# The order of every engine's instructions written by a list schedule

## The chip, the cores and the metric

The kernel runs on one core of one Trainium2 chip. The metric is the device time of one execution in microseconds; of three executions the median is given, with the lowest and the highest. The engines are PE (matmuls and transposes), DVE (the vector engine), ACT (the scalar engine), POOL (GpSimd) and SP, whose queue starts the loads and stores. Each runs its own instructions in its own order and waits for the others by semaphores.

## What is computed

The reference is one layer of a decoder trunk, on 512 tokens of width 1024, all in float32:

```python
mod = silu(c) @ ada_w + ada_b
sh1, sc1, g1, sh2, sc2, g2 = split(mod, 6)
h = rms_norm(x, pre_norm_mix) * (1 + sc1) + sh1
z = h @ w_in                  # g_rnn, x_rnn, q, and keys and values: compressed, selected, window; gates
rnn = gelu(g_rnn) * rg_lru(conv4(x_rnn))                   # two block-diagonal gates, a scan over the tokens
att = nsa_attention(q, ...)                                # 8 heads, 2 groups of keys, three soft-maxes per head
y = concat(rms_norm(rnn), rms_norm(att)) @ w_out
x = x + (1 + g1) * rms_norm(y, post_norm_mix)
h = rms_norm(x, pre_norm_mlp) * (1 + sc2) + sh2
y = square(relu(h @ w_ff1)) @ w_ff2                        # width 4096
x = x + (1 + g2) * rms_norm(y, post_norm_mlp)
```

## The kernel before

**Tiles.** Tokens are four tiles of 128. A float32 product of weight and activation is done as three matmuls (`mm3`, line 762): both are split into a high and a low part of float32r, and the product of the two low parts is left out. A weight is loaded raw, its high part is copied by ACT or DVE and its low part subtracted by DVE or POOL (`split_f32`, line 399; `hi_` and `lo_` in the profile). PSUM's eight banks are given out by use: two `f`, three `s`, one `pv`, two `tp` (line 440 on).

**Stages.** The first wave (`first_wave`, line 689) normalizes x and computes the first 768 columns of the projection, the keys. Then come, mixed with one another: the remaining projections x, g, v and q and the compression (`projections`, `compress`, `values`), the recurrent gates (`gates`, line 913) with their sigmoids, exponentials, roots and four scans on DVE (`vector_work`, line 1060; tiles `r`), the attention by units of a query tile and a pair of heads (`att_scores`, line 1194: scores in `s` banks, a maximum on DVE into `mx`, an exponential on ACT into `p`; `att_values`, line 1249: transposes into `tp` and `pt`, products in the `pv` bank, a division on DVE into `tmp`, sums on POOL into `att`), the modulation vectors from ada_w as multiply-adds on DVE (`ada_cols`, line 1041; `ar` rows of 512 KB, `accT`), and the output projection (banks `f`, weights `hi_o`, activations `h` of the recurrent part and `Q` of the attention). A query tile's attention ends in `att_finish` (line 1297), its residual in `residual` (line 1161). Then y is normalized and transposed for the MLP (`turn_h`, line 1331), whose first four up tiles are done in two halves of the tokens (`up_first`, line 1358: half 0 in banks `pv` and `s` before half 1). The other 28 up tiles (`up`) take 24 matmuls each in an `f` bank, ACT's relu and POOL's square. `down_all` keeps eight banks, and its last four tiles of the inner width go token tile by token tile, each ending in a norm and a store.

**Who sets the order.** Every instruction passes through the class `Clocks` (lines 51 to 270), whose helpers are the profile's lines: `mm` L220, `turn` L223, `act` L234, `elem` L255 for DVE and POOL, `zero` L258, `load` L270. It keeps an estimated clock for each engine and, for each tile, when it was last written and read. Each stage is a generator of instructions (`Stream`); `run_streams` (line 291) asks at every step which stream could go first by those clocks, and gives it a step. The clocks also choose between ACT and DVE for copies and between DVE and POOL for low parts. From line 760 on, the instructions so given are only recorded with cost, predecessors and estimated start (`put`, line 147), and three calls of `flush` (line 118) emit them: after attention, after the transition, and at the end. `flush` goes through one heap for all engines, whose key is 0.7 times an instruction's estimated start less 0.3 times the longest chain behind it (`TAIL`). PE's estimated cost is doubled in a window behind an idle one (`pace`, line 203).

The first wave is emitted inside `tc.manual_schedule()` (lines 488 to 759): there each engine's order is the order of emission. Behind line 759 the framework's own scheduler goes over what is emitted and may order it otherwise.

A tile belongs to a ring of its tag with a fixed number of slots (`tile`, line 69); a new tile takes the oldest slot. `ar` has 2, raw weights `RAW_BUFS` = 4. `Weights` (line 316) loads ahead of splits and splits ahead of use.

## Time and profile before

| | |
|---|---|
| times of three runs | 700.12, 702.43, 703.76 us |
| median | 702.43 us |
| span of the profiled execution, first to last instruction | 700.8 us |
| mean granted TensorE clock in it | 0.978 |
| PE busy | 654.4 us, 93% |
| DVE, ACT, POOL busy | 414.2, 267.6, 157.9 us |
| read from HBM | 82.43 MB, 121 GB/s over the span |

The profiled execution's own time is its span, 700.8 us; the median of the runs is 1.6 us above it. PE is busy in nearly all of the span, so time can only be lost where PE waits or works at a lowered granted clock. A row of a timeline gives start and duration in us, engine, line, operation, tile written from tiles read, and in brackets the idle time before it with what ended it. A matmul's record lasts longer than its share of the engine, since successive ones overlap; distances from start to start are the price. A float32 matmul shows as two records.

### The profile page before, as it was taken

The numbers are of one execution on the slowest core, as the hardware profiler recorded it, in microseconds if no ns is written. First come the engines' busy times: TensorE is split into PE (matmuls) and PEld (weight loads), VectorE is DVE, ScalarE is ACT, GpSimd is POOL, SyncE is SP. The second block draws the span as 40 slices with busy tenths as digits, with TensorE's granted clock in tenths as the row PEclk, the third lists the DMA queues.
The fourth block names the chain that finished last, engine by engine and source line by source line (L and its number), as shares of the span: only waits on it lengthen the run. The fifth ranks groups of instructions, "written<-read, shape, count | busy, mean of one in ns | idle before, by whom it ended". The sixth has DMA issues, their size and how long they took to land.

```text
span 700.8 us, 9072 instructions
## 1 busy us (share of the span) xinstructions
PE 654.4 (93%) x3350; PEld 543.0 (77%) x3350; DVE 414.2 (59%) x788; ACT 267.6 (38%) x553; POOL 157.9 (23%) x148
## 2 busy tenths in 40 slices
PE   3888899894999999998899999999999999999995
PEld 3666788474888889897898888888888888888884
DVE  5998974678688856684895374343353333333334
ACT  4335424584686665565441111111122332222221
POOL 4232010337225201222234343333410000000001
PEclk9999999897999999999999999999999999999999
DMA  8985668642435510001556353432323222223102
GB/s 272 271 249 158 181 206 235 206 130 85 132 111 157 201 35 27 1 0 55 157 151 180 90 151 93 118 91 91 102 97 101 91 91 90 91 91 96 55 18 102
DMA packets 89971, 85.10 MB, mean 121 GB/s; under 512 B 5172, under 2 KB 71876, under 8 KB 89928
## 3 DMA queue, kind: packets, MB, share of 16 engines
q1 hardware_dynamic: 89928, 84.54, 39.6%
q8 instruction: 26, 0.43, 0.3%
q14 instruction: 17, 0.14, 0.1%
HBM read 82.43 MB, written 2.10 MB: 121 GB/s over the span
## 4 chain that ended last, share of the span: by engine, by line
PE 49%; DVE 1%; ACT 0%; issue 0%; POOL 0%; DVEq 0%; POOLq 0%
PE f L220 28%; PE s L220 11%; PE tp L220 7%; PE pv L220 4%; DVE r L255 1%; PE tp L223 0%; ACT ar L234 0%; POOL stat L255 0%; ACT r L234 0%; DVEq L1483 0%; POOLq L1483 0%; DVE h2l L255 0%; DVE stat L255 0%
## 5 line engine op out<-in xcount | busy, mean ns | idle before, releaser
L220 PE MATMUL f<-h,hi_f 128*128 128x512 f32 x224 | 83.4, 393 | 0.0
L220 PE MATMUL f<-h,lo_f 128*128 128x512 f32 x224 | 82.7, 389 | 0.0
L220 PE MATMUL f<-h2l,hi_f 128*128 128x512 f32 x224 | 82.6, 389 | 0.0
L255 POOL TENSOR_TENSOR fT<-fT 128x512 f32<-128x512 f32 x32 | 57.9, 1812 | 107.3 <-ACT fT L234 107.3
L255 DVE TENSOR_TENSOR fl<-fT,fh 128x512 fp32r<-128x512 f32 x28 | 19.3, 690 | 88.1 <-ACT fh L234 88.1
L234 ACT ACTIVATE fT<-f 128x512 f32<-128x512 f32 x28 | 16.8, 600 | 126.1 <-PE f L220 126.1
L234 ACT ACTIVATE fh<-fT 128x512 fp32r<-128x512 f32 x28 | 17.7, 632 | 105.1 <-PE f L220 103.3
L255 POOL TENSOR_SCALAR stat<-stat 128x1 f32<-128x1 f32 (+1 forms) x21 | 7.8, 373 | 218.7 <-DVE stat L255 182.3
L255 DVE CAST hi_f<-raw_f 128x1024 fp32r<-128x1024 f32 x24 | 18.0, 749 | 63.5 <-PE f L220 63.5
L234 ACT ACTIVATE p<-p,mx 128x32 f32<-128x32 f32 (+4 forms) x96 | 45.3, 473 | 26.1 <-DVE mx L255 25.9
L255 DVE SCALAR_TENSOR_TENSOR accT<-ar,sil,accT 128x512 f32<-128x512 f32 x56 | 50.0, 892 | 6.5 <-DMA ar<-in_ada_w 5.9
L255 DVE TENSOR_TENSOR lo_d<-raw_d,hi_d 128x1024 fp32r<-128x1024 f32 x32 | 40.2, 1255 | 15.7 <-ACT hi_d L234 15.3
L220 PEld LDWEIGHTS f<-h,hi_f 128*128 128x128 f32 x224 | 42.1, 188 | 9.1 <-issue 0.5
L220 PEld LDWEIGHTS f<-h2l,hi_f 128*128 128x128 f32 x224 | 42.0, 188 | 9.1 <-issue 0.5
L220 PEld LDWEIGHTS f<-h,lo_f 128*128 128x128 f32 x224 | 42.1, 188 | 8.8
L220 PEld LDWEIGHTS pv<-V,pt 128*128 128x128 f32 x320 | 44.8, 191 | 2.9 <-ACT pt L234 0.5
L220 PE MATMUL pv<-V,pt 128*128 128x64 f32 x320 | 44.4, 260 | 0.2 <-ACT pt L234 0.2
L220 PE MATMUL s<-K,Q 128*128 128x288 f32 (+4 forms) x128 | 35.3, 346 | 9.5 <-DVE mx L255 9.5
L255 DVE TENSOR_TENSOR lo_f<-raw_f,hi_f 128x1024 fp32r<-128x1024 f32 x30 | 40.7, 1357 | 3.9 <-ACT hi_f L234 1.3
L223 PE MATMUL tp<-ident,p 128*128 128x128 f32 (+1 forms) x192 | 40.6, 279 | 0.7 <-DVE h L255 0.7
L220 PE MATMUL s<-hi_d,fh 128*128 128x512 f32 x84 | 33.3, 396 | 0.0
L220 PE MATMUL s<-hi_d,fl 128*128 128x512 f32 x84 | 33.3, 396 | 0.0
(259 smaller groups left out, 1607.4 us busy)
## 6 DMA issues: line engine op xcount, KB each, us to landing
ar<-in_ada_w SPq DMA_DIRECT2D x32, 512.0 KB, 5.4
raw_f<-in_w_ff SPq DMA_DIRECT2D x32, 512.0 KB, 4.1
raw_d<-in_w_ff SPq DMA_DIRECT2D x32, 512.0 KB, 3.2
p<-in_ada_w SPq DMA_DIRECT2D x32, 256.0 KB, 3.8
raw_o<-in_w_out SPq DMA_DIRECT2D x8, 512.0 KB, 4.3
r<-in_x SPq DMA_DIRECT2D x7, 512.0 KB
raw_a<-in_w_in SPq DMA_DIRECT2D x8, 320.0 KB, 5.2
raw_x<-in_w_in SPq DMA_DIRECT2D x4, 512.0 KB
```

What stands on the lines that cost most here:

```text
L220: lambda: self.nc.tensor.matmul(out, lhs, rhs, start=start, stop=stop))
L223: self.issue("pe", out.free_size() / 1175, [out], [src], lambda: self.nc.tensor.transpose(out, src, ident))
L234: lambda: self.nc.scalar.activation(out, src, func, scale=scale, bias=bias, **kw))
L255: self.issue(eng, cost, outs, ins, lambda: fn(out, *args, **kw))
```

## The change

The framework's scheduler is shut out for the whole program: `start_ctx.close()` moves from behind the first wave to the end. `flush` becomes an event-driven list schedule. For each engine (PE, ACT, DVE, POOL, DMA) it keeps a time; at each step the engine that can start first takes, of its instructions whose predecessors are done by the plan, the one with the longest chain behind it. A result is seen by another engine after a lag (`LAG`: 0.2 us from PE, 0.15 from the others, 2.0 for a load). On ACT an instruction that needs another table is put back by `TABLE_COST` = 40 us of chain, and costs 1.3 us more. The plan's times go on from one flush to the next. The costs are set anew, `pace` goes. A raw tile is `live` from its load to its split (or drop), and a new tile takes the first slot in the ring that isn't live; only an instruction that writes a tile depends on the slot's previous user. `run_streams`, the streams, the matmuls and the sizes of tiles stay. In the built order ACT loads its tables 14 times, and a few low parts (`lo_x2`, `lo_v1`) pass from POOL to DVE. In the changed file the helpers' lines are mm L252, turn L255, act L266, elem L287, zero L290, load L304.

```diff
-WINDOW = 4096 / 1200.0
+LAG = {"pe": 0.2, "act": 0.15, "dve": 0.15, "pool": 0.15, "dma": 2.0}
+TABLE_COST = 40.0
...
+        self.emitted = 0
+        self.live = set()
+        self.real = dict.fromkeys(("pe", "act", "dve", "pool", "dma"), 0.0)
+        self.real_table = None
+        self.fin = {}
...
-            old = ring.pop(0)
+            old = ring.pop(next(k for k, v in enumerate(ring) if v not in self.live))
...
     def flush(self):
-        nodes, self.nodes = self.nodes, []
-        tail = [0.0] * len(nodes)
-        for k in range(len(nodes) - 1, -1, -1):
+        first, nodes = self.emitted, self.nodes
+        self.emitted = n = len(nodes)
+        tail, left = {}, {}
+        after = {k: [] for k in range(first, n)}
+        for k in range(n - 1, first - 1, -1):
             eng, cost, prev = nodes[k][:3]
-            tail[k] += cost
+            tail[k] = tail.get(k, 0.0) + cost
+            left[k] = 0
             for j in prev:
-                lag = (SYNC if nodes[j][0] != eng else 0.0) + (DMA_LAT if nodes[j][0] == "dma" else 0.0)
-                tail[j] = max(tail[j], tail[k] + lag)
-        left = [0] * len(nodes)
-        after = [[] for _ in nodes]
-        for k, (_, _, prev, _, _, _) in enumerate(nodes):
-            left[k] = len(prev)
-            for j in prev:
-                after[j].append(k)
-        key = [(1 - TAIL) * start - TAIL * tail[k]
-               for k, (_, _, _, _, start, _) in enumerate(nodes)]
-        heap = [(key[k], k) for k in range(len(nodes)) if not left[k]]
-        heapq.heapify(heap)
-        while heap:
-            _, k = heapq.heappop(heap)
+                if j >= first:
+                    left[k] += 1
+                    after[j].append(k)
+                    tail[j] = max(tail.get(j, 0.0), tail[k] + self.lag(nodes[j][0], eng))
+        ready = {k: max([0.0] + [self.fin[j] + self.lag(nodes[j][0], nodes[k][0]) for j in nodes[k][2] if j < first])
+                 for k in range(first, n)}
+        soon = {e: [] for e in self.real}
+        wait = {e: [] for e in self.real}
+        for k in range(first, n):
+            if not left[k]:
+                heapq.heappush(wait[nodes[k][0]], (ready[k], k))
+        for _ in range(n - first):
+            best = None
+            for e, t in self.real.items():
+                if soon[e]:
+                    at = t
+                elif wait[e]:
+                    at = max(t, wait[e][0][0])
+                else:
+                    continue
+                if best is None or at < best[0]:
+                    best = at, e
+            at, e = best
+            while wait[e] and wait[e][0][0] <= at + 0.01:
+                _, k = heapq.heappop(wait[e])
+                heapq.heappush(soon[e], (-tail[k], k))
+            if e == "act":
+                k = self.pick_act(soon[e], nodes)
+            else:
+                _, k = heapq.heappop(soon[e])
+            cost, func = nodes[k][1], nodes[k][4]
+            if func in TABLES and self.real_table not in TABLES[func]:
+                self.real_table = TABLES[func][0]
+                cost += 1.3
+            self.real[e] = self.fin[k] = at + cost
             nodes[k][3]()
             for j in after[k]:
+                ready[j] = max(ready[j], self.fin[k] + self.lag(e, nodes[j][0]))
                 left[j] -= 1
                 if not left[j]:
-                    heapq.heappush(heap, (key[j], j))
-        self.uses, self.before = {}, {}
+                    heapq.heappush(wait[nodes[j][0]], (ready[j], j))
+    def pick_act(self, soon, nodes):
+        def rank(item):
+            func = nodes[item[1]][4]
+            return item[0] + TABLE_COST * (func in TABLES and self.real_table not in TABLES[func]), item[1]
+        item = min(soon, key=rank)
+        soon.remove(item)
+        heapq.heapify(soon)
+        return item[1]
+    @staticmethod
+    def lag(a, b):
+        return LAG[a] if a != b else 0.0
 
...
     def put(self, eng, cost, outs, ins, fn):
         if self.nodes is None:
@@ -150,10 +197,9 @@
         n, prev = len(self.nodes), set()
         for ap, wr in [(a, False) for a in ins] + [(a, True) for a in outs]:
             key = ap.tensor.name
-            if key not in self.uses:
-                self.uses[key] = []
-                for u in self.uses.get(self.before.get(key), ()):
-                    prev.add(u[5])
+            self.uses.setdefault(key, [])
+            if wr:
+                prev.update(u[5] for u in self.uses.get(self.before.get(key), ()))
             p0, p1, lo, hi = self.box(ap)
             psum = ap.space == PSUM
             for u in self.uses[key]:
@@ -162,10 +208,11 @@
                     prev.add(u[5])
             self.uses[key].append((p0, p1, lo, hi, wr, n, eng))
         prev.discard(n)
-        self.nodes.append((eng, cost, prev, fn, self.start, self.name))
-
-    def issue(self, eng, cost, outs, ins, fn):
+        self.nodes.append((eng, cost, prev, fn, self.func, self.name))
+    def issue(self, eng, cost, outs, ins, fn, func=None):
         start = self.free[eng]
+        self.func = func
         for ap, wr in [(a, False) for a in ins] + [(a, True) for a in outs]:
             key = ap.tensor.name
             psum = ap.space == PSUM
@@ -180,10 +227,7 @@
                     if b[6] != eng or (psum and b[7] != eng and b[5] > b[4]):
                         t += SYNC
                     start = max(start, t)
-        if eng == "pe":
-            cost = self.pace(start, cost)
         end = start + cost
-        self.start = start
         self.put(eng, cost, outs, ins, fn)
         self.free[eng] = end
         done = end + (DMA_LAT if eng == "dma" else 0.0)
@@ -200,38 +244,26 @@
                         b[5], b[7] = done, eng
         return end
 
-    def pace(self, start, cost):
-        k = int(start / WINDOW)
-        if self.windows.get(k - 1, 0.0) < 0.5 * WINDOW:
-            cost *= 2
-        end = start + cost
-        while start < end:
-            stop = min(end, (k + 1) * WINDOW)
-            self.windows[k] = self.windows.get(k, 0.0) + stop - start
-            start, k = stop, k + 1
-        return cost
-
...
     def mm(self, out, lhs, rhs, start, stop):
         n = out.free_size()
-        fast = 1 if rhs.dtype == F32R and n >= 256 else 4
-        self.issue("pe", max(n * fast / 2400 + 0.002, 0.1 if fast == 4 else 0.05), [out], [lhs, rhs],
+        cost = n / 2400 + 0.0133 if rhs.dtype == F32R else max(n / 600 + 0.2, 0.222) if n > 128 else 0.222
+        self.issue("pe", cost, [out], [lhs, rhs],
                    lambda: self.nc.tensor.matmul(out, lhs, rhs, start=start, stop=stop))
 
     def turn(self, out, src, ident):
-        self.issue("pe", out.free_size() / 1175, [out], [src], lambda: self.nc.tensor.transpose(out, src, ident))
+        self.issue("pe", 0.109, [out], [src], lambda: self.nc.tensor.transpose(out, src, ident))
 
     def act(self, out, src, func, scale=1.0, bias=0.0, accum_out=None):
         ins = [src] + [a for a in (scale, bias) if not isinstance(a, float)]
         outs = [out] + ([accum_out] if accum_out is not None else [])
-        cost = 0.05 + out.free_size() / 1200 + 0.043 * (src.space != PSUM) + 0.05 * (len(ins) + len(outs) - 2)
+        cost = 0.051 + out.free_size() / 1200 + 0.058 * (src.space != PSUM) + 0.093 * (len(ins) + len(outs) - 2)
         if func in TABLES and self.table not in TABLES[func]:
             self.table = TABLES[func][0]
             self.free["act"] += 1.3
         kw = {} if accum_out is None else {"accum_out": accum_out}
         self.issue("act", cost, outs, ins,
-                   lambda: self.nc.scalar.activation(out, src, func, scale=scale, bias=bias, **kw))
+                   lambda: self.nc.scalar.activation(out, src, func, scale=scale, bias=bias, **kw), func)
 
...
-            cost = 0.165 + n / (480 if len(wide) > 1 else 1000)
+            cost = 0.165 + n / (350 if len(wide) > 1 else 1000)
...
-        self.issue("dma", out.free_size() * out.shape[0] * 4 / 360000.0, [out], [src],
+        run = min(src.ap[-1][1], out.ap[-1][1]) * 4
+        rate = 300e3 if run <= 512 else 350e3 if run <= 1024 else 385e3
+        self.issue("dma", max(out.free_size() * out.shape[0] * 4 / rate, 0.05), [out], [src],
                    lambda: self.nc.sync.dma_start(out, src))
...
     def load(self):
         name, _, loads, _ = self.jobs[self.l]
...
         self.loaded[name] = raw
+        self.clk.live.add(raw.tensor.name)
         self.raw_live.append(name)
...
             self.raw_live.remove(name)
+            c.live.discard(raw.tensor.name)
             self.part_live.append(name)
...
     def drop(self, name):
         (self.part_live if self.jobs[self.index[name]][3] else self.raw_live).remove(name)
+        self.clk.live.discard(self.loaded[name].tensor.name)
...
     first_wave()
-    start_ctx.close()
     clk.record()
...
     clk.flush()
+    start_ctx.close()
     ctx.close()
```

## The prediction

> **What bounds the kernel now.** I read the page's head first, then the busy time by stage, then the waits, and last the chain of waits.
>
> ```profile
> span 700.8 us, 9072 instructions
> PE 654.4 (93%) x3350; PEld 543.0 (77%) x3350; DVE 414.2 (59%) x788; ACT 267.6 (38%) x553; POOL 157.9 (23%) x148
> ```
>
> PE works 654.4 of 700.8 us, so 46.4 us of idle time and whatever it runs at a lowered clock are all that an order can win. Where they lie is told by the stages (columns: stretch, its length, busy time of PE, weight load, DVE, ACT, POOL, granted clock, DMA share, GB/s):
>
> ```profile
> 60.00:80.00 20.00, 16.18 (x69) 12.65 (x68) 17.70 (x40) 13.32 (x22) 2.39 (x1) 0.91 0.56 155
> ...
> 120.00:140.00 20.00, 17.51 (x58) 10.42 (x57) 13.00 (x16) 12.17 (x16) 5.68 (x4) 0.83 0.60 184
> ...
> 160.00:180.00 20.00, 10.53 (x62) 9.99 (x61) 16.84 (x53) 8.60 (x33) 10.47 (x6) 0.74 0.27 80
> ...
> 320.00:340.00 20.00, 16.95 (x99) 14.04 (x98) 13.13 (x24) 10.82 (x21) 7.26 (x8) 0.91 0.32 96
> 340.00:360.00 20.00, 19.37 (x162) 19.00 (x161) 16.39 (x29) 8.74 (x15) 3.98 (x4) 1.00 0.45 134
> 360.00:680.00 320.00, 320.00 (x1393) 260.90 (x1393) 131.13 (x135) 67.47 (x95) 57.99 (x33) 1.00 0.32 100
> ```
>
> The MLP (360 to 680) keeps PE busy for 320.00 of 320 us at clock 1.00: nothing is to be had there, only lost. What can be won lies in four places: the end of the first wave, the gates (120 to 140), the scan (160 to 180), and the way from attention to the MLP (320 to 360). The first wave's own idle time keeps its order in both kernels. The waits of PE from 100 to 370 us (us in total, times, longest) name them:
>
> ```profile
> PE s L220 <- DVE mx L255: 9.5, 1, 9.5
> ...
> PE pv L220 <- DVE h2l L255: 1.5, 1, 1.5
> PE tp L223 <- POOL att L255: 1.1, 1, 1.1
> ```
>
> The chain of waits agrees: from 361 us to the end it is PE alone, in pieces such as
>
> ```profile
> 355.18 5.88 PE s L220 x49
> 361.06 45.59 PE f L220 x201
> ```
>
> which also give two prices: 45.59/201 = 0.227 us for a matmul of 512 columns, 5.88/49 = 0.12 us for a short one.
>
> **The change, part by part.** It removes no matmul and no vector work; it settles the order on every engine, which the framework's scheduler chose before from line 759 on. An engine then waits at its next instruction even if a later one could go. I followed the built order of the changed kernel with durations from before's rows. Sums are made against the span of 700.8; the median of 702.43 stands 1.6 above it, and I carry this 1.6.
>
> *End of the wave.* PE's first work behind the wave is now the compression (19 matmuls on the evacuated keys) and no longer the projection on Q, so one more evacuation stands ahead of it:
>
> ```profile
> L255 DVE TENSOR_TENSOR K<-s,K 64x512 fp32r<-64x512 f32 x4 | 2.8, 689 | 0.1
> ```
>
> Cost +0.7 us (ends 0 and +2, two more of them with their semaphores).
>
> *The gates.* Before loses 20 - 17.51 = 2.5 us idle and, at clock 0.83, some 3.0 us of PE's work. After, the same sigmoids, tanhs and evacuations stand on ACT in an order that loads tables 14 times, not 11:
>
> ```profile
> L234 ACT ACT_TABLE_LOAD x11 | 14.1, 1283 | 0.9 <-PEq L1476 0.7
> ```
>
> Three loads of 1.28 are 3.9 us more on ACT there; V, g2 and g3 stand behind the gates as cover and not beside them. I take 0, with the ends -5.5 (all of it goes) and +3.9 (all loads show).
>
> *The scan.* The biggest hole, in DVE's and PE's rows:
>
> ```profile
> 156.78 8.75 DVE L255 TENSOR_TENSOR_SCAN r<-p,r 128x512 f32<-128x512 f32 x4 [1.17 <-POOL r L255]
> 165.45 1.68 DVE L255 SCALAR_TENSOR_TENSOR accT<-ar,sil,accT 128x512 f32<-128x512 f32 x1
> 167.06 2.28 DVE L255 TENSOR_TENSOR lo_q<-raw_q,hi_q 128x1024 fp32r<-128x1024 f32 x1
> ...
> 169.93 0.61 PE L220 MATMUL s<-K,Q 128*128 128x288 f32 x1 [9.47 <-DVE mx L255]
> ```
>
> Four scans (8.75), a multiply-add (1.68) and a split (2.28) stand ahead of the reductions that free a score bank; PE waits 9.47 us, and at the stage's clock of 0.74 it loses some 0.26 x 10.53 = 2.7 more. Together 12.2 us. After, DVE's order is scan, split, scan, five reductions, scan, two reductions, scan. The first release comes two scans (4.4), the split (2.28) and some 0.9 of reductions behind the first scan's start: 7.6 us, where before took 169.93 - 156.78 = 13.1. So PE waits 9.5 - 5.5 = 4.0. Then the two other scans and reductions (6 us) and an exponential stand ahead of the next transposes, with 17 short matmuls of V, 4 of scores and 5 two-pass ones of values as cover (31 passes, 3.7 us): another 3.0. (The plan prices a scan at 0.065 + 512/930 = 0.62, against 2.19 here, so this wait is not in the plan.) With 1.7 for the lowered clock (a share of the 2.7 as 7.0 is of 9.5, less what the break in two gives back) the hole costs 8.7: **-3.5 us** (ends -9 and +2).
>
> A rule of the Trainium skill bears on those 1.7 and on the short waits below. The page "TensorE: Matmul & The Clock Gate", Part 1, says that the clock falls to half after an idle window of about 3.4 us and comes back after as much sustained work. By it the waits of 4.0 and 3.0 might cost none or one such window, 0 to 1.7 us, and waits of a microsecond none; in the row for 320 to 340 the clock is 0.91 although the waits there are those of 1.1 and 1.5 above, so the trace is less lenient than that rule.
>
> *Attention, first half.* Here I expect the new loss. In the built order DVE's stretch from the evacuation behind the scan to the one ahead of the selected units stands beside PE's stretch between the same tiles. PE: 76 matmuls of 512 columns at 0.227 (17.3), 214 short passes at 0.12 (24 of V, 48 two-pass value products, 40 scores, 54 transposes: 25.7), 1.6 of small ones: 44.6 us. DVE: 137 instructions, among them 20 multiply-adds of the modulation (accT), 5 splits, 33 reductions. Before's row for such a stretch, with one multiply-add:
>
> ```profile
> 180.00:240.00 60.00, 59.30 (x363) 50.24 (x361) 47.05 (x140) 42.32 (x129) 20.48 (x23) 1.00 0.54 166
> ```
> ```profile
> 204.31 0.75 DVE L255 SCALAR_TENSOR_TENSOR accT<-ar,sil,accT 128x512 f32<-128x512 f32 x1
> ```
>
> There 140 DVE instructions take 47.05 us, 0.336 each, beside 59.30 of PE, which is hardly ever short. 137 of nearly the same mix make 46 to 47. After, DVE thus has the greater sum: the list gives each engine whatever is ready, so the multiply-adds come early and the output projection, PE's filler, later. PE loses at least 46 - 44.6 = 1.4. Followed wait by wait, it stands at a score bank behind two multiply-adds (0.8), at Q2 (1.0), at an exponential (1.0), at a value bank (0.5), twice 0.4, and at a transposed tile behind 2.6 us of multiply-adds (1.3): 5.4. Before lost 0.7 here. **+4.7 us** (ends -0.7 and +12).
>
> *Attention, second half.* Behind it come the units of the third query tile without filler: PE 24 by the same prices, DVE 21, each handing to the other. I take **+1.5** (ends 0 and +4). With the output projection as filler again, PE has some 69 us beside 43 of DVE: 0.
>
> *From attention to the MLP.* Before: 20 - 16.95 = 3.05 us idle (1.1 and 1.5 of it the waits above), 0.63 idle in 340 to 360, and 0.09 x 16.95 = 1.5 by the clock of 0.91: 5.2 us. Its last residual chain ran beside work that could go ahead:
>
> ```profile
> 334.17 0.74 DVE L255 SCALAR_TENSOR_TENSOR r<-f,stat,r 128x512 f32<-128x512 f32 x1
> ...
> 335.66 1.07 ACT L234 ACTIVATE ar<-r 128x1024 f32<-128x1024 f32 x1
> ...
> 337.74 0.61 POOL L255 TENSOR_TENSOR stat<-stat,nhalf 128x1 f32<-128x1 f32 x1
> ...
> 341.95 1.28 DVE L255 SCALAR_TENSOR_TENSOR r<-r,stat,r 128x1024 f32<-128x1024 f32 x1
> ...
> 345.37 0.75 DVE L255 TENSOR_SCALAR r<-r,stat 128x1024 f32<-128x1024 f32 x1 [2.14 <-POOL stat L255]
> ...
> 346.18 0.88 PE L223 MATMUL tp<-ident,r 128*128 128x128 f32 x6 [0.50 <-DVE r L255]
> ```
>
> That is 346.18 - 334.17 = 12.0 us from product to transpose. After, the chain (two products 1.5, square 1.3, power 0.9, two multiplies 1.4, sum 1.3, square 1.3, power 0.8, scaling 0.75, with hops and three other DVE results between) takes 9.7 us behind the last output product. But PE has put the chain's transposes behind only 12 transposes and 23 short matmuls (4.1 us), and 60 matmuls of the first up tiles, ready by then, stand behind them: a wait of 5.6, in two parts. Ahead of it the last attention tile's transposes stand with no cover (1.9, where before had 1.1), and the clock falls once (1.5, as before). Together 9.0: **+3.8 us** (ends -3 and +6).
>
> *Up and down.* Same matmuls, banks in the same pairs in up, eight in turn in down, ACT, DVE and POOL under half busy: 0 (ends 0 and +4; PE's full row above leaves no gain).
>
> Sum: 0.7 + 0 - 3.5 + 4.7 + 1.5 + 3.8 = +7.2. 700.8 + 7.2 = 708.0, and with 1.6: **709.6 us**.
>
> **The rivals.** (a) *The list closes the holes.* It hands PE whatever is ready with the longest tail, and costs are nearer to the rows (0.227 for a matmul is planned as 0.2266). If DVE keeps ahead in attention, the scan's hole shrinks to 3 and the way to the MLP costs 2: -9.2 - 3.2 - 0.5 from the gates = -12.9, 689.5 us. For it: before's hole is plainly a matter of order. Against: the scan's price, and 46 us of DVE beside 44.6. It decides if DVE's sum in that stretch stays below PE's. (b) *A wash.* The attention terms vanish, since each wait I count there is under 1.4 us and the prices are rounded, and the rest (0.7 - 3.5 + 3.8) leaves +1: 703.4. That the order isn't carried out as planned would end here too. (c) *Loads block DVE.* In order, a multiply-add that waits for its row stops the reductions behind it:
>
> ```profile
> ar<-in_ada_w SPq DMA_DIRECT2D x32, 512.0 KB, 5.4
> ```
>
> The plan counts 2.0 + 0.52 MB / 385 GB/s = 3.4 us, 2.0 less than this. If a third of that shows for the 10 such loads of the stretch, it is +6.7, and with a fallen clock (1.5 to 2.7 above) +9: 718.6.
>
> **How the numbers follow.** My forecast has 0.40 (its own range 706 to 714), (a) 0.25, (b) 0.20, (c) 0.15. Half a per cent, 3.5 us, is about what a measurement can tell from no change: faster 0.25, same 0.20, slower 0.55. The range goes from 690, with some half of (a) below, to 722, past (c)'s price: about 0.18 is left out.
>
> **What would show it.** Right: PE waiting on DVE and ACT in many pieces of 0.3 to 1.5 us between the scan and the third query tile, where before has one wait; a wait of 4 to 6 us on DVE's h or r just ahead of the MLP; a scan hole of two parts, 4 and 3; the MLP at 320 of 320. Wrong: PE at 100% through attention, or the MLP's stretch no longer full, which would move the end by more than all the other terms.

## The result, and the profile after

The changed kernel takes 721.45 us (median of 720.79, 721.05, 721.86 and 724.11) beside 702.55 for the kernel before in the same rounds: the ratio is **1.0285, 95% interval 1.0256 to 1.0315**, slower. The forecast was 709.6, +7.2 us; it came out at +18.9, inside the range and far from the value. Below, "after" is the changed kernel and "before" the old one. In after's profile L252 is the matmul helper, L255 the transpose, L266 the activation, L287 DVE's and POOL's helper.

The head of after's page (PE's line has the busy time and its share of the span):

```profile
span 718.8 us, 9079 instructions
...
PE 665.9 (93%) x3350; PEld 550.5 (77%) x3350; DVE 429.9 (60%) x796; ACT 269.3 (37%) x550; POOL 143.8 (20%) x146
```

The number of matmuls is the same 3350, yet PE is busy for 11.5 us more than before's 654.4, and idle for 718.8 - 665.9 = 52.9 us, 6.5 more than 46.4. Together 18.0, the whole difference of the spans (718.8 against 700.8). Equal work that takes longer is work at a lowered clock: **the loss is 11.5 us of clock and 6.5 us of idle time.** The stages of after, with the columns of the prediction's table, tell where:

```profile
60.00:80.00 20.00, 16.24 (x76) 14.65 (x76) 15.39 (x26) 13.58 (x22) 3.31 (x2) 0.78 0.54 164
80.00:100.00 20.00, 20.00 (x96) 16.90 (x96) 16.97 (x33) 4.90 (x7) 0.00 (x0) 0.88 0.81 252
120.00:140.00 20.00, 15.59 (x86) 10.94 (x85) 10.00 (x20) 15.07 (x27) 1.27 (x1) 1.00 0.67 186
160.00:180.00 20.00, 15.06 (x97) 14.16 (x96) 15.72 (x39) 12.52 (x34) 12.92 (x10) 0.83 0.24 81
200.00:220.00 20.00, 18.07 (x102) 15.73 (x100) 17.14 (x60) 14.13 (x49) 10.66 (x12) 0.78 0.37 109
220.00:240.00 20.00, 19.18 (x110) 15.83 (x109) 14.57 (x40) 9.26 (x32) 3.22 (x8) 0.88 0.42 131
320.00:340.00 20.00, 17.84 (x103) 14.78 (x102) 11.60 (x29) 10.78 (x26) 6.61 (x12) 0.91 0.00 1
340.00:360.00 20.00, 14.92 (x103) 13.92 (x102) 16.79 (x28) 9.94 (x17) 7.87 (x6) 0.83 0.39 106
360.00:680.00 320.00, 317.96 (x1433) 258.31 (x1432) 149.22 (x144) 72.27 (x98) 53.36 (x34) 1.00 0.34 107
```

Idle time is the length less PE's first number; the clock's loss is that number times (1 - granted clock). The granted clock of a row is a mean over all of its length, waits too, so a sum over rows of 2 us comes out somewhat otherwise; figures of the clock below that no shown row gives are such sums. In 200 to 240, where before ran at 1.00, after loses 1.9 + 0.8 idle and 4.0 + 2.3 by the clock (6.8 by rows of 2 us). The MLP is no longer quite full: 317.96 of 320. PE's waits in after:

```profile
PE s L252 <- DVE mx L287: 4.9, 1, 4.9
PE tp L255 <- DVE h L287: 4.8, 1, 4.8
PE s L252 <- DVE r L287: 3.8, 1, 3.8
PE f L252 <- ACT r L266: 3.4, 3, 1.9
PE tp L252 <- DVE accT L287: 2.4, 1, 2.4
PE tp L255 <- POOL att L287: 2.2, 1, 2.2
PE s L252 <- DVE Q L287: 1.9, 1, 1.9
```

Before's list is led by 9.5 us on mx, and what follows is short; after's has seven names of 1.9 to 4.9 us. The longest, on mx, is the scan's, at half its old length, for the reason that the prediction gave. DVE's rows there (start, duration; five reductions stand between the second scan and the third), and POOL's:

```profile
161.44 2.29 DVE L287 TENSOR_TENSOR_SCAN r<-p,r 128x512 f32<-128x512 f32 x1 [1.19 <-POOL r L287]
163.65 2.22 DVE L287 TENSOR_TENSOR lo_q<-raw_q,hi_q 128x1024 fp32r<-128x1024 f32 x1
165.79 2.28 DVE L287 TENSOR_TENSOR_SCAN r<-p,r 128x512 f32<-128x512 f32 x1
...
168.96 1.21 DVE L287 TENSOR_TENSOR_SCAN r<-p,r 128x512 f32<-128x512 f32 x1
```
```profile
158.59 8.39 POOL L287 TENSOR_TENSOR r<-r,r 128x512 f32<-128x512 f32 x4 [9.58 <-DVE r L287]
```

A scan took 2.28 and 2.29 us while POOL multiplied beside it, and 1.21 and 1.18 with POOL idle (166.98 to 170.25 and 171.53 to 173.17); all four scans of before stand beside one run of POOL's multiplies (152.96 to 170.47). So the hole is also as long as POOL makes it.

By stage, idle and clock together, before then after, the forecast's change and the measured one:

| stage | before | after | forecast | measured |
|---|---|---|---|---|
| end of the wave (60 to 100) | 5.3 | 9.8 | +0.7 | +4.4 |
| gates (100 to 160) | 6.9 | 8.1 | 0 | +1.1 |
| scan (160 to 180) | 12.2 | 7.5 | -3.5 | -4.6 |
| attention (180 to 320) | 1.0 | 9.3 | +6.2 | +8.4 |
| attention to MLP (320 to 380) | 5.2 | 11.9 | +3.8 | +6.7 |
| up to down | 0 | 1.5 | 0 | +1.5 |

(Each entry comes from the rows of the stage in both traces as above; rounding leaves 0.1 to 0.2, and 0.5 us lie in stretches not listed.)

### The profile page after: what moved, and what is told of

Its sections match the earlier page's. It is cut to its first block, busy times and chain, and to the rows that moved or that the text cites. A ratio compares the mean times of both kernels' runs of the same rounds, so it can differ in the third digit from the quotient of the medians.

```text
span 718.8 us, 9079 instructions
## 1 busy us (share of the span) xinstructions
PE 665.9 (93%) x3350; PEld 550.5 (77%) x3350; DVE 429.9 (60%) x796; ACT 269.3 (37%) x550; POOL 143.8 (20%) x146
## 4 chain that ended last, share of the span: by engine, by line
PE 72%; DVE 14%; DMA 4%; issue 3%; ACT 3%; POOL 2%; SPq 1%; DVEq 0%; POOLq 0%; ACTq 0%
PE f L252 37%; PE s L252 16%; PE pv L252 8%; PE tp L252 7%; DVE accT L287 6%; PE tp L255 3%; DMA ar<-in_ada_w 2%; DVE r L287 2%; ACT r L266 1%; DMA r<-in_x 1%; DVE h L287 1%; DVE p L287 1%; POOL stat L287 1%; DMA raw_x<-in_w_in 1%; SPq L304 1%
## 5 line engine op out<-in xcount | busy, mean ns | idle before, releaser
L252 PE MATMUL f<-h,hi_f 128*128 128x512 f32 x224 | 73.1, 396 | 0.6 <-ACT hi_f L266 0.6
L287 POOL TENSOR_TENSOR fT<-fT 128x512 f32<-128x512 f32 x32 | 50.5, 1597 | 111.7 <-ACT fT L266 111.7
L287 DVE TENSOR_TENSOR fl<-fT,fh 128x512 fp32r<-128x512 f32 x28 | 20.8, 743 | 86.2 <-PE f L252 86.0
L252 PE MATMUL f<-h,lo_f 128*128 128x512 f32 x224 | 72.2, 392 | 0.0
L252 PE MATMUL f<-h2l,hi_f 128*128 128x512 f32 x224 | 71.6, 390 | 0.0
L266 ACT ACTIVATE fT<-f 128x512 f32<-128x512 f32 x28 | 16.8, 598 | 126.8 <-PE f L252 126.8
L266 ACT ACTIVATE p<-p,mx 128x32 f32<-128x32 f32 (+4 forms) x96 | 45.5, 474 | 35.2 <-DVE mx L287 35.0
L287 DVE CAST hi_f<-raw_f 128x1024 fp32r<-128x1024 f32 x24 | 25.9, 1077 | 53.5 <-PE f L252 53.5
L252 PEld LDWEIGHTS pv<-V,pt 128*128 128x128 f32 x320 | 51.0, 200 | 5.6 <-issue 0.4
L287 DVE SCALAR_TENSOR_TENSOR accT<-ar,sil,accT 128x512 f32<-128x512 f32 x56 | 46.1, 823 | 13.7 <-DMA ar<-in_ada_w 12.4
L287 POOL TENSOR_SCALAR stat<-stat 128x1 f32<-128x1 f32 (+1 forms) x21 | 8.7, 415 | 224.9 <-DVE stat L287 178.2
L252 PEld LDWEIGHTS f<-h,hi_f 128*128 128x128 f32 x224 | 42.0, 188 | 14.0 <-ACT fT L266 3.9
L287 DVE TENSOR_TENSOR lo_d<-raw_d,hi_d 128x1024 fp32r<-128x1024 f32 x32 | 41.7, 1304 | 18.0 <-ACT hi_d L266 17.4
L287 DVE TENSOR_TENSOR lo_f<-raw_f,hi_f 128x1024 fp32r<-128x1024 f32 x30 | 44.1, 1480 | 11.8 <-ACT hi_f L266 8.9
L252 PE MATMUL pv<-V,pt 128*128 128x64 f32 x320 | 50.2, 266 | 0.0
L252 PEld LDWEIGHTS f<-h,lo_f 128*128 128x128 f32 x224 | 42.0, 188 | 9.2 <-issue 0.2
L252 PE MATMUL s<-K,Q 128*128 128x256 f32 (+4 forms) x128 | 41.9, 386 | 6.9 <-DVE mx L287 4.9
L252 PEld LDWEIGHTS f<-h2l,hi_f 128*128 128x128 f32 x224 | 42.1, 188 | 7.8
L266 ACT ACTIVATE hi_d<-raw_d 128x1024 fp32r<-128x1024 f32 x28 | 29.8, 1063 | 41.1 <-PE f L252 41.1
L255 PE MATMUL tp<-ident,p 128*128 128x128 f32 (+1 forms) x192 | 44.0, 287 | 0.5 <-ACT p L266 0.4
L266 ACT ACTIVATE fh<-fT 128x512 fp32r<-128x512 f32 x28 | 17.7, 632 | 70.5 <-PE f L252 69.4
L287 POOL TENSOR_TENSOR r<-r,r 128x512 f32<-128x512 f32 x12 | 18.6, 1565 | 84.0 <-ACT r L266 69.5
```

The source lines that it names most:

```text
L252: lambda: self.nc.tensor.matmul(out, lhs, rhs, start=start, stop=stop))
L255: self.issue("pe", 0.109, [out], [src], lambda: self.nc.tensor.transpose(out, src, ident))
L266: lambda: self.nc.scalar.activation(out, src, func, scale=scale, bias=bias, **kw), func)
L287: self.issue(eng, cost, outs, ins, lambda: fn(out, *args, **kw))
```

## The experiments

The theories at the start: **T1**, a few waits of 2 to 5 us remain and the clock that falls behind them is the loss; **T2**, the strict order as such costs the time; **T3**, the list's order does, whoever issues it; **T4**, durations that the plan has wrong cause the waits. Ratios are to before, timed in the same rounds, with 95% intervals; 0.01 is 7.0 us.

### Strict order or list: e1, e2

e1 is after with the strict order ended where before ended it; e2 is before with the strict order held to the end.

```diff
     first_wave()
+    start_ctx.close()      # e1 adds this to after; e2 takes it from before
     clk.record()
...
     clk.flush()
-    start_ctx.close()      # e1 takes this from after; e2 adds it to before
     ctx.close()
```

> The kernel after, with the strict order ended behind the first wave, as before had it: the list decides the order of emission, and the framework's scheduler is free to deviate from it. T1 (a few waits in order, and the clock that falls behind each of them, are the loss): the scheduler lets PE take the next free matmul at some of these waits, so 705 to 713 us, with fewer us at a granted clock of 0.5. T2 (it is the strict order as such that costs the time): 700 to 705, as before. T3 (the list's order and its new prices are at fault, whoever issues it): 718 to 724, as after.

> The kernel before, with its own recording, prices and sorting, but the strict order held to the end: the other half of the change alone. T2 (strict order as such): 715 us or more, as after. T3 (the list's order): 700 to 706, as before. T1: the old order was never meant to be followed to the letter, so it waits in other places: 708 to 720, and its loss lies in waits of over 1.5 us with the granted clock at 0.5 behind them, not in many waits under 1 us.

e1: 718.19 us, ratio 1.0228 (1.0184 to 1.0272), at after's edge: freeing the scheduler is worth some 4 us of 20, and the two intervals just overlap. e2: 762.47, ratio 1.088 (1.0847 to 1.0912): T2 had said 715 or more, but no theory had 60 us. Its waits are of another kind than after's:

```profile
PE pv L220 <- ACT pt L234: 11.5, 6, 5.5
PE tp L223 <- ACT p L234: 7.9, 4, 3.0
```

The old sorting leaned on the scheduler for 60 us; the list needs it for 4. T2 is true of the old order and nearly false of the new one. By e1 the list with its prices carries most of after's loss.

### The clock by itself: e3, e5

Two small kernels: stretches of one kind of matmul, with or without a pause of PE ahead of each.

```diff
# e3, (kind, count, additions on DVE in the pause ahead): a pause of some 4.2, 3.0 or 1.8 us for 2, 1, 0
+    plan = [(long, 90, 0), (long, 90, 2), (short, 60, 2), (long, 90, 2), (mid, 140, 2), (long, 90, 2), (wide, 60, 2),
+            (long, 90, 2), (mix, 70, 2), (long, 90, 0), (long, 90, 0), (short, 60, 0), (long, 90, 1), (long, 90, 1),
+            (short, 60, 1), (long, 90, 0)]
# e5, None: no pause
+    plan = [(long, 60, None), (short, 110, None), (long, 60, None), (turn, 110, None), (long, 60, None),
+            (mixture(2), 110, None), (long, 60, None), (mixture(3), 110, 2), (long, 60, None), (mixture(4), 110, 2),
...
```

> Not the kernel: it leaves out the whole computation and writes zeros. It has sixteen stretches of matmuls on the same operands, of one kind each (512 columns in f32r; 256 columns in f32r; 64 columns in f32; 128 columns in f32; a mixture of 2 of 512 columns to 5 of 64), with pauses of PE of about 4.2, 3.0 or 1.8 us between them. T1 (behind a pause the clock comes back late where the work is short f32 passes): after a pause of 4.2 us the first 4 to 5 us of the 512-column stretches run at half clock, as in the attention of before, while 64-column passes stay at half clock for 12 us or more, and the mixture lies between. Rival (the recovery takes the same time whatever the work): 4 to 5 us for each kind. On the pause: if a wait of 1.9 us is enough, as it looked in the attention of after, stretches behind 1.8 us show half clock too; if not, only those behind 3.0 and 4.2 us do.

> Not the kernel: it leaves out the whole computation and writes zeros. Stretches of matmuls again. First without any pause: 64-column f32 passes, 128-column transposes, and a mixture of 2 matmuls of 512 columns to 5 passes, each behind a stretch of 512 columns. Then, each behind a pause of about 4.2 us, mixtures of 3, 4 and 5 of 512 columns in 7, transposes, and f32 matmuls of 288 columns. e3_clock showed that 64-column passes and the mixture of 2 in 7 keep the clock at half for as long as they run. Theory T1 as it stands (the clock falls behind a wait, and passes only fail to bring it back): without a pause the granted clock stays at 1.00 in all three stretches; behind a pause the mixtures of 4 and 5 in 7 come back within 8 us, transposes and 3 in 7 don't. Rival (short passes count as idle themselves): the clock falls to 0.5 within 4 to 8 us of the start of the 64-column stretch, with no wait at all.

PE's windows in e3 (length, busy, granted clock): 512 columns behind 4.36 us, 64 columns behind 3.63, 512 columns behind 1.83, and 64 columns behind 1.21:

```profile
32.00:36.00 4.00, 2.91 (x7) 0.50 0.00 0
36.00:40.00 4.00, 4.00 (x16) 0.80 0.00 0
60.00:64.00 4.00, 4.00 (x20) 0.50 0.00 0
80.00:84.00 4.00, 4.00 (x21) 0.50 0.00 0
272.00:276.00 4.00, 3.00 (x13) 1.00 0.01 2
292.00:296.00 4.00, 2.79 (x18) 1.00 0.00 0
296.00:300.00 4.00, 4.00 (x25) 0.62 0.00 0
```

And in e5: 64 columns with no pause, within the stretch; 3 of 512 columns in 7 behind 4.36 us, at its start and its end; 4 in 7 behind 4.35:

```profile
24.00:28.00 4.00, 4.00 (x38) 1.00 0.02 4
132.00:136.00 4.00, 4.00 (x15) 0.50 0.00 0
172.00:176.00 4.00, 4.00 (x17) 0.50 0.00 0
196.00:200.00 4.00, 3.95 (x14) 0.57 0.00 0
200.00:204.00 4.00, 4.00 (x27) 1.00 0.00 0
```

Matmuls of 512 columns bring the clock back in 4.5 us here, and in 3.2 to 5.9 in the eight such stretches that began at half; 256 columns in f32r took 5.4 us and 128 columns in f32 5.9. 64-column passes never do: half clock from the first to the last of 25.86 us. Of mixtures, 2 in 7 (in e3) stay at half for all of their 30 us, where I had expected something in between, 3 in 7 for 46 us, and 4 in 7 are back within 4. Without a pause nothing falls, in 24.67 us of 64-column passes. And a pause too short to matter among 512-column matmuls (1.83 us, clock 1.00) is enough among short passes: behind 1.21 us the clock fell 2 us after they began (0.62 in 296 to 300 is full speed for the first 1 us), and stayed there; behind 2.46 us it did the same. Among 512-column matmuls it fell behind 3.10 us. Each of these pauses was seen once from full clock. So the mechanism of T1 is shown in the small kernels, and it fits after's wait of 1.9 us among short attention work.

Transposes behind a pause were not measured (that stretch had no operand that kept it waiting), and f32 matmuls of 288 columns kept 1.00 behind 3.72 us, which this picture doesn't explain. The Trainium skill's page "TensorE: Matmul & The Clock Gate", Part 1, which the prediction weighed, counts sustained work without asking of what kind; these rows differ, and they decide.

### One wait at a time: e4, e6, e7, e8

Each mends one place of after's list and leaves the rest nearly as it was. For e4 and e6 a bonus in the ranking:

```diff
-                heapq.heappush(soon[e], (-tail[k], k))
+                heapq.heappush(soon[e], (-tail[k] - nodes[k][5], k))
# e4: 500 for the matmuls of x0.  e6: 500 for q_evac's instructions
# e7
-            split_f32(c, hi, lo, raw[:, :n])
+            split_f32(c, hi, lo, raw[:, :n], name in ("f0", "f1", "f2", "f3"))
# e8
+            if what == "tensor_tensor_scan":
+                cost = n / 233
```

> The kernel after, with one change to the list: the 24 matmuls of x0 (512 columns, f32r) get a bonus in PE's ranking and so stand ahead of all but 9 of the compression's matmuls, instead of behind 38 of them. PE does the same work in both, and waits for the same first evacuation. T1 (what the wave's end lost is the clock, which stays at half for 14 us while short f32 passes run behind the wait): the clock is back within 5 us, and 3 to 5 us go: 716 to 718.5. Rival (the loss there is the wait itself, or the clock recovers at its own time): within 1 us of after, 720.5 to 722.5.

> The kernel after, with one change to the list: the evacuations of the Q projections rank first on ACT and DVE, so that the low parts of Q2 and Q3 stand on DVE ahead of the multiply-adds of the modulation (accT) and the reciprocals, and not behind them. T1 (a wait of 1.9 us on Q and the 14 us at half clock behind it cost 8.2 us together): both go, 711 to 716 us, of which some 6 us are clock. Rival (idle time is what counts, and the multiply-adds will be waited for elsewhere): 0 to 2 us, 719.5 to 722.

> The kernel after, with the low parts of the first four up tiles (f0 to f3) subtracted on DVE; after has two of them on POOL, in the middle of the last residual chain. T4 (a price is missing from the plan: POOL's subtraction of 2.4 us holds back the chain's power on POOL, and the second one stretches DVE's multiply-add beside it from 1.28 to 3.35 us): DVE's operation takes 1.3 us, the wait on h falls from 4.8 us to 1 or 2, and 3 to 6 us go with its clock: 715 to 718.5. Rival (T3: the list has put the last transposes too early on PE, whatever the chain takes; the two subtractions only move to DVE, 1.2 us each): 720 to 722.5.

> The kernel after, with one price of the plan put right: a scan of 512 columns at 2.2 us on DVE, as the rows have it, for 0.62. T4 (mispriced durations cause the waits): the list puts reductions ahead of scans, and the scan's hole (4.9 us idle and 2.6 by the clock) loses half or more: 716 to 718.5. T3 (the list's order waits somewhere anyway, since its slack is below what the rows scatter): within 2 us of after, 719.5 to 723, with the hole smaller and a new wait in the gates or in attention.

| | us | ratio |
|---|---|---|
| e4, x0 first | 721.99 | 1.0309 (1.0261 to 1.0357) |
| e6, Q first | 719.21 | 1.0264 (1.0229 to 1.0299) |
| e7, low parts on DVE | 719.44 | 1.0274 (1.0227 to 1.032) |
| e8, scan's price | 721.31 | 1.0277 (1.0216 to 1.0337) |

All four intervals overlap after's; T1's and T4's numbers fail in all of them, though three of the edits did locally what they were to do. In e4 the clock's loss at the wave's end falls from 6.5 to 3.3 us, and idle time grows from 0.7 to 3.1 in the 28 us up to the gates (100 to 128 us in after, 4.5 later in e4) and from 4.9 to 6.3 in the scan (its profiled execution was its slowest, 728.57). In e6 the wait on Q is gone and one of 1.48 us on mx stands 2 us later, with 3.4 us of clock behind it for 6.8. e8 moved the wait from the scores to the projection of V (6.2 on its weight, lo_v). In e7 DVE's operation in the last residual chain is short again. After, the stretched instruction with POOL's subtraction beside it, and e7's:

```profile
346.92 3.35 DVE L287 SCALAR_TENSOR_TENSOR r<-r,stat,r 128x1024 f32<-128x1024 f32 x1
```
```profile
346.86 2.33 POOL L287 TENSOR_TENSOR lo_f<-raw_f,hi_f 128x1024 fp32r<-128x1024 f32 x1
```
```profile
345.81 1.28 DVE L287 SCALAR_TENSOR_TENSOR r<-r,stat,r 128x1024 f32<-128x1024 f32 x1 [0.72 <-POOL stat L287]
```

The wait on h falls from 4.8 to 3.35, and from 320 us to the MLP the clock takes 4.1 us for 3.6. So a single wait was not what to mend.

### Waits filled with dead matmuls: e9, e10, e17, e12

Matmuls whose result is never read, in front of a matmul that waits, keep the wait and take away the pause. The order of the other instructions is unchanged (in e9, e10, e17).

```diff
+    def fill(self, warm):
...
+            for _ in range(warm[2]):
+                self.nc.tensor.matmul(warm[0], warm[1][:, :P], warm[1], start=True, stop=True)
...
                     mm(ps[:, :n], Q[h][:, tok(i)], K1[g][:, c0:c0 + n], True, False,
+                       (ps, K1[0][:, 0:512], 8) if (h, i) == (2, 0) else None)
```

(The last line is e17's; e10's has h 0.)

> The kernel after, in the same order, with matmuls of 512 columns whose result is never read put in front of four waiting matmuls of PE: 15 at the end of the wave, 20 ahead of the scores in the scan, 8 ahead of the scores on Q0, 9 between the last attention transposes. They need nothing that the waiting matmul waits for, and at 0.227 us each they take 3.4, 4.5, 1.8 and 2.0 us, within the waits of 3.8, 4.9, 1.9 and 2.2 us. The waits stay: nothing in the real work comes earlier by the order. T1 (it is the clock that is lost behind the waits): the 6.5, 2.5, 6.6 and 1.3 us that these four places lose by the lowered clock go, less what doesn't fit: 704 to 709 us. Rival (the loss is the idle time and the order, and the lowered clock hides in waits that would be there anyway, since PE then only waits longer at the next wait): 714 to 722.

> The kernel after, in the same order, with the 8 matmuls in front of the scores on Q0 alone. T1: the wait of 1.9 us there stays and the 14 us at half clock behind it go: 5 to 7 us less than after, 714 to 717. Rival (the later waits take it back): 719.5 to 722.

> The kernel after, in the same order, with 8 never-read matmuls of 512 columns in front of the scores on Q2 for the first query tile, which wait 1.9 us for DVE's low part; e9_fill and e10_fill_q had them at Q0, whose low part had long been there, so that they were only 1.8 us more work. T1: the 6.8 us that after loses here by the clock go, and the units behind it run ahead on filler: 4 to 7 us less than after, 714.5 to 717.5. Rival, as e9_fill showed at the wave's end (PE then waits for DVE, ACT or a load a little later, and the time is back): the clock's loss goes from the stretch of 208 to 232 us, but idle time of 2 us or more appears behind it, 719 to 722.

> The kernel before, with the framework's scheduler, and matmuls that are never read: 14 ahead of x0 and 62 ahead of the scores that wait for the scans (it places 39 of them in that hole of 9.5 us, 23 around the gates). T1: before loses 1.7 us by the clock at the wave's end, 3.2 in the gates and 2.8 behind the scan; filled, most of that goes, less some 2.5 us of the 23 that don't fit in the gates' waits: 696 to 700 us, below both kernels. Rival (the filled time was needed, or the waits only grow): 702 to 706.

e9: 724.06, ratio 1.0294 (1.027 to 1.0317); no gain, and past the rival's 722 too. The clock did what T1 said and the time came back. PE from 72 to 156 us, after and then e9:

```profile
72.00:100.00 28.00, 28.00 (x132) 0.77 0.72 221
100.00:128.00 28.00, 27.28 (x153) 1.00 0.41 113
128.00:156.00 28.00, 22.36 (x88) 0.94 0.75 211
```
```profile
72.00:100.00 28.00, 25.99 (x150) 1.00 0.74 219
100.00:128.00 28.00, 24.59 (x127) 0.94 0.44 114
128.00:156.00 28.00, 23.34 (x88) 0.82 0.68 195
```

The 6.4 us of clock are gone; in their place stand 2.0 us of idle ahead of 100, 3.4 and 1.7 ahead of 128, and 4.9 of clock in the gates for 1.7. PE had run ahead to weights that were not there. Rows of e9:

```profile
105.36 1.24 DVE lo_g L300
106.61 3.90 DMA raw_g<-in_w_in
110.60 1.06 ACT hi_g L279
112.19 6.90 PE f L263 x22
```

DVE's late split of g frees the buffer, then the load, then ACT. In after, without the fill, the same four start at 105.21, 106.47, 110.20 and 111.79: what PE won did not move them. So from the wave to the gates the stretch is set by DVE and by the loads behind it, and the clock's loss at the wave's end lies in time that would be waited anyway. (The 4.9 in the gates are not all the fill's doing: e17, which has none there, lost 5.1. From the first compression matmul to V's first, e9 took 85.9 us, and the unfilled after, e17 and e10 84.3, 85.0 and 85.8.)

e10: 725.44, ratio 1.0315 (1.0295 to 1.0336), a miss of mine: its 8 matmuls stood at Q0, and the wait is on Q2, so they were 1.8 us of extra work (in e9 too). e17 has them at Q2: **718.30, ratio 1.0217 (1.019 to 1.0245)**, 3.1 us less by the medians, 4.8 by the ratios, between its two forecasts. After and e17:

```profile
208.00:232.00 24.00, 22.07 (x111) 0.72 0.47 152
```
```profile
208.00:232.00 24.00, 23.92 (x151) 1.00 0.61 189
```

Here the 6.8 us of clock go from this stretch. The fill itself costs nothing, as it stands in the wait: from the last output product ahead of it to the scores it is 2.54 us, 2.55 in after. Some comes back a little later, 1.7 by the clock behind a wait of 1.2 us. From that product to the first output product on Q it is 80.4 us for 84.9 in after, so 4.5 are saved. So the clock is a cost of its own in attention, where T1 holds, and none at the wave's end, where it falls.

e12, the same for before: 703.75, ratio 1.0017 (1.0002 to 1.0031), against 696 to 700. It takes 11 us of waits and 4 of clock away and pays with 76 matmuls, 17.2 us; 23 of them (5.2 us) stand around the gates, where before's longest wait is 2.5 us. T1's number fails here.

### Prices: e11, e13, e15, e16, e18, e19

```diff
# e13 (e11: also ACT, POOL and loads; e15: e11 with the scheduler free; e16: before with the new ones)
-        cost = n / 2400 + 0.0133 if rhs.dtype == F32R else max(n / 600 + 0.2, 0.222) if n > 128 else 0.222
+        fast = 1 if rhs.dtype == F32R and n >= 256 else 4
+        cost = max(n * fast / 2400 + 0.002, 0.1 if fast == 4 else 0.05)
# e18, e19
+        cost *= {"dve": 1.17, "act": 1.21}.get(eng, 1.0)
+        cost *= {"pe": 0.81}.get(eng, 1.0)
```

> The kernel after, with its list, its ring of tiles and its strict order, but the prices of matmuls, transposes, activations, POOL and loads as they were before (a 512-column matmul 0.215, a 64-column pass 0.109, a transpose 0.109, loads at 360 GB/s). T4 (the new prices are what misleads the list): below 716. T3 (a list in strict order waits wherever reality is slower than its plan, by any prices): within 3 us of after or slower, 719 to 735, since old prices stand further from the rows.

> The kernel after with the old prices of PE alone (matmuls and transposes); activations, POOL and loads keep the new ones. e11_old_prices showed that all old prices together take 10.5 us off. If PE's prices carry it (with the old ones a two-pass matmul counts 0.109 for 0.222, so PE is planned faster than it is, and what waits on DVE and ACT is planned behind more of the 512-column work): 709 to 713. If the prices of loads, POOL and ACT carry it (a load of 0.5 MB planned at 3.4 us after, 3.5 before, so nearly the same): 718 to 722. If any change of prices just draws another order of the same quality: anywhere from 708 to 724.

> The kernel after with its list and ring of tiles, the old prices, and the framework's scheduler free behind the first wave: of the change, only the sorting is left. If the prices cost 10.5 us and the strict order 4, each by itself: 705 to 708, within 1 per cent of before, and the sorting by the list costs the rest, 3 to 5. If the strict order is harmless with old prices: 709.5 to 712.5, as e11_old_prices.

> The kernel before with the new prices alone: old sorting by start and tail, the clock's halving still planned, the framework's scheduler. If the new prices do harm by themselves, whatever sorts: 708 to 718. If they only harm the list, which trusts them to the letter: 700 to 705.

> The kernel after, with DVE's prices times 1.17 and ACT's times 1.21, PE's new ones kept. In the list from the wave's end to the last output product the plan adds up to 220.5 us for PE, 165.9 for DVE and 125.3 for ACT; the trace of after has 254.3 x 0.92 = 234 at full clock, 193.7 and 151.3 from 71 to 342 us. So PE is priced 6 per cent low, DVE 17, ACT 21; with the old prices PE's sum is 179, 31 per cent low. T5 (what matters is the price of DVE and ACT against PE's: the new prices raised PE's alone, so the list counts on DVE and ACT being done before they are): 707 to 713, as with the old prices of PE. Rival T6 (the old prices were better by chance, or for their low price of short passes): 717 to 724.

> The kernel after, with all of PE's new prices times 0.81, so that their sum is that of the old ones (179 us) and their proportions stay the new ones (a two-pass matmul 0.180, one of 512 columns 0.184). T5 (the sum of PE against DVE and ACT decides): 708 to 713. T6 (the old proportions decide, a short two-pass matmul half as dear as one of 512 columns): 717 to 724.

| sorting | prices | scheduler free behind the wave | strict |
|---|---|---|---|
| old | old | before, 1 | e2, 1.088 |
| old | new | e16, 1.0085 (1.0062 to 1.0108) | - |
| list | old | e15, 1.0095 (1.0061 to 1.013) | e11, 1.0117 (1.0102 to 1.0132) |
| list | old for PE alone | - | e13, 1.0124 (1.0086 to 1.0162) |
| list | new | e1, 1.0228 (1.0184 to 1.0272) | after, 1.0285 (1.0256 to 1.0315) |
| list | new, DVE and ACT raised | - | e18, 1.0205 (1.0179 to 1.0231) |
| list | new, PE times 0.81 | - | e19, 1.007 (1.0043 to 1.0097) |

In microseconds of 702.5: the new prices cost 6.0 with the old sorting and 11.8 with the list and the strict order; the list with old prices and a free scheduler (and with the new ring of tiles, and without `pace`, which no run takes apart) costs 6.7; the strict order costs the list 1.5 (old prices) to 4.0 (new), differences as small as their intervals. It is PE's prices that matter: e13 gives all that e11 does. So T3's number for e11 (719 to 735) is wrong, and T4 holds in a form that I had not meant: the new prices are **nearer** to the rows and the order made by them is worse. e19 keeps the new proportions, makes PE 19% cheaper in the plan, and comes to 707.32 (the best of the strict orders). That speaks for T5, PE's price against the other engines', and against T6's proportions. e18, which raises DVE and ACT to the trace instead, wins only 5.6 us by the ratio (e19 15.1, e13 11.3), in T6's range and not in T5's. So: cheap PE in the plan gives a better order in every pair that was run, and why raising the others does only a third to a half as much stays open (POOL's, the loads' and the hops' times were not raised with them).

One thing goes along with it: ACT loads its tables, at 1.28 us each, 14 times in after and 12 in e18, but 8 times in e13 and e19 and 7 in e11 and e15. No run holds that number fixed, so whether it is part of the cause is not shown; e1, with 18, is no slower than after. Three stretches of PE, from 72, 208 and 320 us, in after and then in e19:

```profile
72.00:156.00 84.00, 77.64 (x371) 0.90 0.63 182
208.00:260.00 52.00, 48.95 (x304) 0.87 0.29 91
320.00:380.00 60.00, 52.19 (x347) 0.91 0.16 44
```
```profile
72.00:156.00 84.00, 81.00 (x409) 0.92 0.50 148
208.00:260.00 52.00, 51.89 (x315) 1.00 0.53 162
320.00:380.00 60.00, 55.00 (x342) 0.97 0.34 98
```

These three are better, and attention is nearly whole again; the scan between them is not (160 to 180 loses 4.7 idle and 3.6 by the clock, for 4.9 and 2.5 in after). No version here beats before.

## Why the prediction was right or wrong

The direction was right (slower 0.55), and the idle time too: its terms hold +8.2 us of idle (0.7 - 2.5 + 6.2 + 3.8) and -1.0 of clock (the scan's 2.7 to 1.7); measured were **+6.5 idle and +11.5 clock**. The whole miss is the clock. **The step that failed is the price of a wait**: outside the scan, every wait was priced at its own length, and no stage got more lowered clock than before. By rows of 2 us, before and then after, the clock took 1.7 and 6.6 us at the wave's end, 0 and 6.8 in attention, and 1.7 and 3.6 on the way to the MLP; in the gates and the scan together, 5.9 and 4.2.

- *End of the wave, +0.7; measured +4.4.* The wait is 3.76 us, where before had 3.82: the "one more evacuation" cost nothing. Mis-sized was what runs behind it. The step saw that compression now comes first and counted no clock for it; 38 passes of 64 columns then ran at half clock, which lasted from 71.2 to 84.9 us. By e9 the time would mostly have been lost in the gates otherwise.
- *Gates, 0; measured +1.1.* Five waits of 0.4 to 2.5 us for three of 0.5 to 2.5, less clock. Within its ends.
- *Scan, -3.5; measured -4.6.* Right in its mechanism: scan, split, scan, then the reductions. One wait of 4.9 came and not 4.0 and 3.0: V's matmuls covered the second, and the last two scans, taken at 2.19 each from before's rows, took 1.2 beside an idle POOL.
- *Attention, +4.7 and +1.5; measured +8.4.* **Here the failed step shows most plainly.** The prediction counted seven small waits that add up to 5.4, each at its own length and with no clock behind it, although it had noted itself that before's clock was low behind waits of 1.1 and 1.5. There was one of 1.9 us, on Q2 behind the multiply-adds as followed, one of 1.1, and 6.8 us of clock behind the first. So the idle time grew by 2.1 and not by 6.2, DVE was no busier from 180 to 320 us than in before (100.1 and 101.1 us), and that the sums, 6.2 and 8.4, lie near each other is luck. e3 shows how it comes: among short passes a wait of 1.2 us was enough for the clock to fall, and they didn't bring it back. The second half cost next to nothing.
- *Attention to MLP, +3.8; measured +6.7.* The two waits, 2.2 and 4.8, were forecast as 1.9 and 5.6. The clock fell twice and not once, and took 3.6 us for the 1.5 forecast.
- *Up and down, 0; measured +1.5.* One wait on g2row at the start of down, not followed in the order; inside the ends of that term. (The MLP's stretch no longer full was named as a sign of being wrong that would outweigh all other terms; it did not, at 1.5 us.)
- *Rivals.* (a) held that prices nearer to the rows speak for the list; e11, e13 and e19 showed the reverse. (c), loads that block DVE, gave nearly the measured time by another cause: DVE waits for ar 12.4 us in after and 5.9 before, but behind the first wave no wait of PE on those multiply-adds is longer than 2.5.

What the runs leave as the cause: the list by itself some 7 us, the new prices 6 to 12 more (with the list, PE's alone carry it), the strict order 1.5 to 4; by e15, e11 and after in turn, 6.7, 1.5 and 11.8 add up to the 20.0 of the ratio. In the trace more than half of it appears as half clock behind waits of 2 to 5 us, of which only the part in attention is shown to be time that can be won back (e17). Left open: why a plan with PE too cheap sorts better.

## What to carry to other kernels

Price a wait of TensorE with what runs behind it: in front of short passes 1.9 us of waiting lost 8.7 (after, 208 to 232 us), in front of 512-column matmuls 1.83 us lost 1.83 (e3), so long matmuls are the better ones to put right behind a wait. Then ask whether the stage is TensorE's at all, since clock saved where DVE and the loads set the pace bought nothing (e4, e9). And this planner wasn't improved by correcting one engine's prices: time the order that it makes, with the others' prices as they stand.

## What the runs showed of the hardware

- The granted clock stays at half for as long as short work runs: 25.86 us of 64-column f32 passes, 46 us of 3 in 7 matmuls of 512 columns; 4 in 7 bring it back within 4 us (e3, e5).
- The same short work without a pause keeps the full clock for 24.67 us (e5).
- DVE and POOL stretch one another: a scan of 512 columns on DVE took 2.29 us beside POOL's multiplies and 1.21 with POOL idle, and those multiplies 2.1 us each (8.39 for 4) beside scans and split, 1.28 beside reductions (after); a multiply-add of 1024 columns on DVE took 3.35 us beside a subtraction on POOL of 2.33, and 1.28 with that gone (after, e7).
